# Modulation by blocks of 128 features, three weight tiles multiplied while they load, and other numbers in the planner

## The chip, the cores and the metric

One core of a Trainium2 chip runs the whole kernel. The metric is device time in microseconds (us), the median of three timed runs of one launch. The engines are TensorE (PE: matmuls; PEld: its weight loads), VectorE (DVE), ScalarE (ACT), GpSimd (POOL) and SyncE (SP), which here issues every transfer, on one queue.

## The reference, cut to what matters

One inference step of a hybrid decoder layer: 512 prompt tokens and 8 x 4 sample tokens, 544 columns in all, model width 1024.

```python
def layer_front(x, c, w_cond, b_cond, w_in):
    shift, scale, gate = jnp.split(jax.nn.silu(c) @ w_cond + b_cond, 3, axis=-1)
    h = x * (1 + scale[:, None]) + shift[:, None]
    return gate, split_columns(h @ w_in)
```

`c` has 9 rows: one for the prompt, one for each sample sequence. `w_cond` is 1024 x 3072, `w_in` is 1024 x 11280. The columns of `h @ w_in` feed two branches: windowed softmax attention (24 heads in 3 groups) and a gated delta rule (8 heads: a causal convolution of width 4, silu, a chunked triangular solve, a state that passes through 4 chunks of 128 tokens; its decays and betas, the gates, come from 16 further columns of `w_in`). Then

```python
merged = jax.nn.sigmoid(ga) * (ya @ w_branch_a) + jax.nn.sigmoid(gb) * (yb @ w_branch_b)
r = ALPHA * x + gate * (merged @ w_out)         # then a LayerNorm over the features
```

The kernel also returns the shifted key/value caches, the convolution tails and the delta states.

## The kernel before, in words

**How the work is laid out.** Features lie on the partitions, 8 blocks of 128 (`KT`); tokens are the columns. `h` is kept as a pair: `hhi`, rounded to fp32r, and `hlo`, the rest. Every weight tile (128 output columns of `w_in`, 128 x 1024 in SBUF) is split in the same way into `hi` and `lo` by `split`: a copy on ACT and a subtraction on DVE. A tile's product over one half of the tokens (272 columns) is 8 blocks x 3 matmuls (`hi` with `hhi`, `hi` with `hlo`, `lo` with `hhi`) into one PSUM buffer, so a tile has 48 matmuls. `stream` in `body` goes through the tiles (jobs) in a fixed order: three of delta head 0, nine of attention, and so on. A job's `evac` takes each half out of PSUM. PSUM has 8 buffers: 2 `pp` for the stream, 2 `pd`, 3 `pg`, 1 `pb`.

**The front.** Before any tile, scale and shift must be known. `cond_product` multiplies silu(c) (tile `cs`, 32 columns with 9 in use) with `w_cond`, which comes in 8 transfers of 1 MiB (tile `wc`): first the 4 with the scale columns, then the 4 with the shift columns. `to_features` turns each result (`Y`) into columns over the partitions by small products with a selecting constant (`cst`, result in `pd`). Only then is `h` formed block by block: on DVE `xT` times scale plus shift, on ACT the copy `hhi`, on DVE the difference `hlo`.

**The gates.** `gates` multiplies `h` with the 16 gate columns (32 matmuls of 272 columns into `pg`), brings the result to tokens on partitions (`cg`, `abT`) and computes softplus, exponentials and running sums in some 25 small DVE and ACT instructions on 34 columns; their tiles lie in two pools (`gtab`, `gt`), and the attention's pool `ap` opens only once both are closed.

**What sets the order.** The program is first recorded: `Threads` interleaves the generators (delta rule, delta blocks, gates, attention, stream, sample work) on a clock that counts matmul cost, and each instruction gets a rank. Then `Recorder.schedule` plans it: a list scheduler with costs and latencies for each engine (`cost`, `WAKE`, `margin`), a transfer queue, tile buffers and a model of TensorE's clock; at each step the engine that is free first takes its ready instruction of the lowest rank. What comes out is a fixed order on each engine. All instructions are issued by `emit`, so the profile gives one line, L638, for nearly all of them; they are told apart by their tiles.

**The end of the first phase.** The tiles of the delta rule and of the attention lie in pools (`dl`, `ap`) that are closed after the eighth head's rule. The buffers `zt` of the later gate tiles (`zp`) are opened after that. The delta rule ends, for each head, with a root (`rn`) and a scaling (`orow`) that is written out.

Of the kernel before, what the change touches and what calls it, by code (L numbers as in the profile page):

```python
# [38 lines left out]
EARLY_A, EARLY_B = 7, 2  # L39
S0B = 7  # L40
# [203 lines left out]
class Recorder:  # L244
# [4 lines left out]
    OVER = {"ve": 0.08, "se": 0.10, "ge": 0.05}  # L249
    HOLD = 1.0  # L250
# [3 lines left out]
    def __init__(self):  # L254
        self.ops, self.events, self.rank, self.now, self.idle = [], [], 0, 0.0, 0.0
        self.group = None
        self.scratch = {}
# [8 lines left out]
    def add(self, engine, name, args, kw):  # L266
        op = Op(len(self.ops), engine, name, args, kw, self.rank)
        op.group, op.part, op.epoch = self.group, self.rank, len(self.events)
# [65 lines left out]
    def cost(self, op, args):  # L334
# [5 lines left out]
        op.two = len(tensors) > 1 and not in_psum  # L340
        op.transfer = None
# [18 lines left out]
        elif e == "ve":  # L360
            if op.name == "reciprocal":
                c = 0.15 + 6.25e-3 * n
            elif op.name == "memset":
                c = 0.06 + 0.83e-3 * n
            elif len(tensors) == 1 and not in_psum and op.name in ("tensor_scalar", "tensor_copy"):
                c = 0.15 + 0.76e-3 * n
            else:
                c = 0.152 + 1.05e-3 * n
            op.cost, op.late = c - 0.08, 0.08
        elif e == "se":  # L370
            c = (0.185 if in_psum else 0.21) + 0.83e-3 * n
            a = 0.15 if "accum_out" in op.kw else 0.0
# [42 lines left out]
    def schedule(self):  # L415
# [9 lines left out]
        for op in ops:  # L425
            op.left = len(op.deps)
            for d in op.deps:
# [22 lines left out]
        def candidate(op):  # L450
# [22 lines left out]
            for d, data in op.deps.items():  # L473
# [3 lines left out]
                else:  # L477
                    r = max(r, p.end + (0.06 if data and op.engine != "pe" else 0.0))
            for t in op.tiles:
                if t.ops[0] == op.n:  # L480
# [29 lines left out]
        while done < len(ops):  # L510
# [31 lines left out]
            else:  # L542
                op = None
                if e == "pe" and rounded[0] and not avail[e][0][-1].rounded:

                    if t - min(x[-1].ready for x in avail[e] if not x[-1].rounded) < self.HOLD:
# [5 lines left out]
                if op is None:  # L552
                    op = pop(avail[e])[-1]
            if op.group is not None:
# [7 lines left out]
            if e == "pe":  # L562
# [8 lines left out]
                busy.append((t, t + c))  # L571
            if op.two and e in port:
# [8 lines left out]
            op.done = t + c + op.late  # L581
            free[e] = op.end
# [108 lines left out]
def body(ctx, tc, io):  # L691
# [80 lines left out]
    def cond_rows(part, k0, nk):  # L772
        return io["w_cond"][k0 * 128:(k0 + nk) * 128, part * D:(part + 1) * D].rearrange("(k p) c -> p k c", p=128)

    def to_features(pv, k, rows):

        for i in range(4):
            pe.matmul(pv[:, k + i, 0:9], rows[:, 128 * i:128 * i + 128], C("selc"), start=True, stop=True)

    f16 = lambda t: t[:, :128].rearrange("p (a b) -> p a b", b=16)  # L780
# [10 lines left out]
    gctx = ExitStack()  # L791
    d1 = pool(gctx, "gtab", 1)
    tables["g"] = d1.tile([128, CONST[1].shape[1]], F32, name="cg")
    dta = d1.tile([128, 2, 34], F32, name="dta")
    with ExitStack() as fctx:
        fr = pool(fctx, "front", 1)
        cT = fr.tile([128, KT, 32], F32, name="cT")
        ve.memset(cT, 0.0)
        sp.dma_start(cT[:, :, 0:9], io["cT"])
# [5 lines left out]
        ve.tensor_mul(cs, cT, th)  # L805
        xT = fr.tile([128, KT, NT], F32, name="xT")
        pieces = {}
        for part in (1, 0):
            for k in range(0, KT, 2):
                pieces[part, k] = fr.tile([128, 2, D], F32, name="wc", bufs=8)  # L810
                sp.dma_start(pieces[part, k], cond_rows(part, k, 2))
                if (part, k) == (1, 6):
                    sp.dma_start(cst, io["const"])
        sp.dma_start(wab, io["w_ab"])
        raws[0] = wraw.tile([128, D], F32, name="wt", tag="wraw")
        sp.dma_start(raws[0], io["w_in"][TILE_AT["b", 0, 1]])
        weights[0] = split(raws[0], D, ve)
        for k in range(0, KT, 2):
            sp.dma_start(xT[:, k:k + 2], io["xT"][:, k:k + 2])
# [4 lines left out]
        def load_front(part):  # L824
            for k in range(0, KT, 2):
                for n in range(2):
                    for q in range(2):
                        yield k + q, n, pieces[part, k][:, q, 512 * n:512 * n + 512]

        sc = fr.tile([128, KT, 9], F32, name="sc")  # L830
        sh = fr.tile([128, KT, 9], F32, name="sh")
        for part, t in ((1, sc), (0, sh)):
            ps = [pp(), pp()]
            take(cond_product(part, load_front, ps), 99)
            pv = f16(pd())
            bias = bT[:, 8 * part:8 * part + 8, None].to_broadcast([128, 8, 9])
            for n in range(2):
                Y = fr.tile([128, 512], F32, name="Y", bufs=2)
                if n:
                    se.activation(Y, ps[n], AF.Copy)  # L840
                else:
                    ve.tensor_copy(Y, ps[n])
                to_features(pv, 4 * n, Y)
            if part:
                ve.scalar_tensor_tensor(t, pv[:, :, 0:9], 1.0, bias, op0=OP.add, op1=OP.add)
            else:
                ve.tensor_add(t, pv[:, :, 0:9], bias)
        sp.dma_start(bnw, io["b_norm_w"])
        ve.tensor_scalar(hbnw, bnw, 0.5, None, op0=OP.mult)
        xs = xT[:, :, SEQ:].rearrange("p k (b t) -> p k b t", t=4)  # L850
        per_token = lambda t, k, n: t[:, k:k + n, 1:9, None].to_broadcast([128, n, 8, 4])
        for k in range(0, KT, 2):
            ve.tensor_mul(xs[:, k:k + 2], xs[:, k:k + 2], per_token(sc, k, 2))
# [1406 lines left out]
```

## Time and profile before

| | us |
|---|---|
| median of 3 runs | 984.84 (983.84 to 985.1) |
| the profiled execution's own time | 984.89 |
| its span, first to last instruction | 982.8 |
| busy in the span: PE, PEld | 922.8 (94%), 842.9 (86%) |
| busy: DVE, ACT, POOL | 739.4 (75%), 413.6 (42%), 75.7 (8%) |
| mean granted TensorE clock | 0.980 of full speed |

Times in the rows are from the span's start. Matmul records overlap: a busy matmul shows longer than the distance to the next one, and it is the distance that adds up. An fp32 matmul leaves two records, an fp32r matmul one. "Idle before" is the time for which the engine had nothing to do ahead of a row, with what ended it.

### The profile page before, as it was taken

The numbers are of one execution on the slowest core, as the hardware profiler recorded it, in microseconds if no ns is written. First come the engines' busy times: TensorE is split into PE (matmuls) and PEld (weight loads), VectorE is DVE, ScalarE is ACT, GpSimd is POOL, SyncE is SP. The second block draws the span as 40 slices with busy tenths as digits, with TensorE's granted clock in tenths as the row PEclk, the third lists the DMA queues.
The fourth block names the chain that finished last, engine by engine and source line by source line (L and its number), as shares of the span: only waits on it lengthen the run. The fifth ranks groups of instructions, "written<-read, shape, count | busy, mean of one in ns | idle before, by whom it ended". The sixth has DMA issues, their size and how long they took to land. (4 is left out here: it accounts for less than half of the span.)

```text
span 982.8 us, 20665 instructions
## 1 busy us (share of the span) xinstructions
PE 922.8 (94%) x8070; PEld 842.9 (86%) x8070; DVE 739.4 (75%) x1620; ACT 413.6 (42%) x971; POOL 75.7 (8%) x176
## 2 busy tenths in 40 slices
PE   4899999999999999999999799998999999999896
PEld 1699988999978988888988698798899999997785
DVE  0575565866889999699987866655799899847658
ACT  0364447543546443456443545433342222234420
POOL 0120001101001410000200100001010000000000
PEclk8799999999999999999999999998999999999998
DMA  9676755675877887968777665359689899975513
GB/s 359 206 249 207 218 188 201 215 196 186 290 250 230 264 247 247 311 219 281 267 247 241 206 196 182 134 188 324 249 286 340 322 418 406 352 242 175 189 38 109
DMA packets 106340, 237.76 MB, mean 242 GB/s; under 512 B 30898, under 2 KB 62140, under 8 KB 103556
## 3 DMA queue, kind: packets, MB, share of 16 engines
q1 hardware_dynamic: 106244, 236.45, 71.2%
q8 instruction: 63, 1.03, 0.4%
q14 instruction: 33, 0.27, 0.1%
HBM read 220.40 MB, written 103.70 MB: 330 GB/s over the span
## 5 line engine op out<-in xcount | busy, mean ns | idle before, releaser
L638 PE MATMUL pp<-hhi,hi 128*128 128x272 f32 x1408 | 414.9, 295 | 8.3 <-DVE spare L638 2.6
L638 PE MATMUL pp<-hhi,lo 128*128 128x272 f32 x1408 | 414.1, 294 | 0.0
L638 PE MATMUL pp<-hlo,hi 128*128 128x272 f32 x1408 | 412.1, 293 | 0.6 <-DVE hlo L638 0.6
L638 PEld LDWEIGHTS pp<-hhi,hi 128*128 128x128 f32 x1408 | 268.1, 191 | 12.5 <-DVE spare L638 2.9
L638 PEld LDWEIGHTS pp<-hlo,hi 128*128 128x128 f32 x1408 | 268.0, 190 | 2.5 <-DVE hlo L638 0.9
L638 PEld LDWEIGHTS pp<-hhi,lo 128*128 128x128 f32 x1408 | 267.7, 190 | 2.0 <-issue 1.0
L638 ACT ACTIVATE hi<-wt 128x1024 fp32r<-128x1024 f32 (+1 forms) x104 | 106.7, 1026 | 169.6 <-PE pp L638 148.1
L638 DVE TENSOR_TENSOR lo<-wt,hi 128x1024 fp32r<-128x1024 f32 (+1 forms) x104 | 122.4, 1177 | 63.1 <-ACT hi L638 60.7
L638 DVE SCALAR_TENSOR_TENSOR acc<-ext,cw,acc 128x568 f32<-128x568 f32 x72 | 57.5, 799 | 2.5 <-ACT acc L638 0.9
L638 ACT ACT_TABLE_LOAD x34 | 43.6, 1283 | 12.5 <-DMA cT<-in_cT 7.9
L638 ACT ACTIVATE P<-P,st 128x256 f32<-128x256 f32 (+1 forms) x64 | 31.3, 489 | 34.9 <-DVE st L638 34.8
L638 DVE TENSOR_TENSOR slab<-slab 128x512 f32<-128x512 f32 (+1 forms) x66 | 42.4, 667 | 4.6 <-DMA slab<-in_vs 2.0
L638 DVE TENSOR_REDUCE slab<-slab 128x8 f32<-128x512 f32 (+2 forms) x66 | 42.5, 656 | 0.6 <-ACT slab L638 0.4
L638 ACT ACTIVATE zt<-pp 128x272 f32<-128x272 f32 x48 | 18.6, 388 | 50.8 <-PE pp L638 38.7
L638 POOL COPY cx<-ext 128x3 f32<-128x3 f32 (+1 forms) x48 | 32.4, 704 | 90.8 <-ACT ext L638 90.6
L638 PE MATMUL pp<-ybl,hi 128*128 128x272 f32 x128 | 37.0, 289 | 0.0
L638 PE MATMUL pg<-k,q 64*128 64x128 f32 (+1 forms) x192 | 34.4, 331 | 2.8 <-DVE st L638 2.7
L638 PE MATMUL pp<-ybh,lo 128*128 128x272 f32 x128 | 37.0, 289 | 0.0
L638 PE MATMUL pp<-ybh,hi 128*128 128x272 f32 x128 | 36.8, 287 | 0.0
L638 PEld LDWEIGHTS pg<-k,q 64*128 64x128 f32 x192 | 23.2, 186 | 10.5 <-DVE st L638 4.5
L638 DVE CUSTOM_DVE_ANT_0 P<-pg,bias 128x256 f32<-128x256 f32 (+1 forms) x64 | 24.0, 403 | 8.5 <-PE pg L638 8.4
L638 ACT ACTIVATE ext<-pp 128x272 f32<-128x272 f32 (+2 forms) x72 | 20.0, 315 | 23.2 <-PE pp L638 19.3
(395 smaller groups left out, 1585.0 us busy)
## 6 DMA issues: line engine op xcount, KB each, us to landing
out_kv_s<-in_cache SPq DMA_DIRECT2D x144, 512.0 KB
wt<-in_w_in SPq DMA_DIRECT2D x88, 512.0 KB
out_kv_s<-in_cache SPq DMA_DIRECT2D x24, 496.0 KB
wc<-in_w_cond SPq DMA_DIRECT2D x8, 1024.0 KB
slab<-in_ks SPq DMA_DIRECT2D x32, 256.0 KB
slab<-in_vs SPq DMA_DIRECT2D x32, 256.0 KB
kv<-in_ks SPq DMA_DIRECT2D x16, 512.0 KB
kv<-in_vs SPq DMA_DIRECT2D x16, 512.0 KB
```

What stands on the lines that cost most here:

```text
L638: getattr(real[x.engine], x.name)(*map(arg, x.args), **{k: arg(v) for k, v in x.kw.items()})
```

## The change

Five edits.

1. **The front by feature blocks.** The host lays out the scale and shift columns of `w_cond` as `w_mod`: 8 blocks of 1 MiB, block k holding all 1024 rows of the 128 shift and 128 scale columns of features 128k to 128k+127. Each block is loaded into its own tile `wm`, multiplied (8 matmuls of 256 columns instead of a share of 512-column ones), brought over the partitions by 2 small products and applied to block k of `xT` at once, so `hhi[k]` and `hlo[k]` exist before block k+1 is needed. The input `cT` is padded to 32 columns by the host, and the memset of `cT` goes.
2. **Three tiles between.** The weight tiles of the first three jobs load between the blocks (`FIRST`), are split there, and after each block their 18 matmuls over that block are issued (rank 9). The six halves take both `pp`, all three `pg` and the `pb` buffer. `stream` then only evacuates these jobs. Loads of the next jobs are held back to 28 us on the planner's clock (`BEHIND`).
3. **The gates in borrowed tiles.** The gates' tiles come from the pool `opool` (nine buffers, tag `o`) which the first tiles' weights also borrow; `gtab` and `gt` are gone, and `ap` opens without waiting for the gates. The block of zeros is half as wide and is written in two transfers.
4. **The planner's numbers.** VectorE: 1.045 in place of 1.05 ns per element, and 0.055 us more for an instruction with a per-partition operand and two tensors or for a transpose; ScalarE: 0.155 in place of 0.185 us from PSUM, 0.07 in place of 0.15 for an accumulated output, 0.08 for a per-partition operand; a new wait `AGAIN` between dependent instructions of one engine (0.11 VectorE, 0.14 ScalarE, where it was 0.06).
5. **The planner's rules.** An instruction on a PSUM buffer waits until the other engines' last instruction on that buffer is done (`turn`); a GpSimd copy counts VectorE's hold on the shared port; `hold` becomes a property of an instruction and is 0 for the last block's products.

```diff
+FIRST = (1, 2, 3)
+BEHIND = 28.0
...
+    AGAIN = {"pe": 0.0, "ve": 0.11, "se": 0.14, "ge": 0.11, "sp": 0.0}
...
-                c = 0.152 + 1.05e-3 * n
+                c = 0.152 + 1.045e-3 * n
+            if op.name == "scalar_tensor_tensor" and pointer or op.name == "transpose":
+                c += 0.055
...
-            c = (0.185 if in_psum else 0.21) + 0.83e-3 * n
-            a = 0.15 if "accum_out" in op.kw else 0.0
+            c = (0.155 if in_psum else 0.21) + 0.83e-3 * n
+            a = (0.07 if "accum_out" in op.kw else 0.0) + (0.08 if pointer else 0.0)
...
-                    r = max(r, p.end + (0.06 if data and op.engine != "pe" else 0.0))
+                    r = max(r, p.end + (self.AGAIN[op.engine] if data else 0.0))
...
+                turn = max((d + self.WAKE[e] for b in op.banks for x, d in b.turn.items() if x != e), default=0.0)
+                if turn > t + 0.001:
+                    op.ready = turn
+                    push(wait[e], (turn, op.n))
+                    continue
...
+        wm = [fr.tile([128, KT, 256], F32, name="wm", bufs=6) for _ in range(KT)]
+        for k in range(KT):
+            sp.dma_start(wm[k], io["w_mod"][k])
+            if k == 0:
+                sp.dma_start(cst, io["const"])
+            if k % 2 == 0:
+                sp.dma_start(xT[:, k:k + 2], io["xT"][:, k:k + 2])
+            if k in FIRST:
+                i = FIRST.index(k)
+                raws[i] = wraw.tile([128, D], F32, name="wt", tag="wraw")
+                sp.dma_start(raws[i], io["w_in"][TILE_AT["b", 0, (1, 0, 2)[i]]])
...
+        ahead = {0: [pp(), pp()], 1: [pg(), pg()], 2: [pg(), pb_()]}
...
+        for k in range(KT):
+            pc = pd()
+            rec.hold = 0.0 if k == KT - 1 else rec.HOLD
+            with rec.together():
+                for i in range(KT):
+                    q = i % 4
+                    pe.matmul(pc[32 * q:32 * q + 32, 0:256], cs[:, i, :], wm[k][:, i, :], start=(i < 4), stop=(i >= 4),
+                              tile_position=(0, 32 * q))
+            Y = fr.tile([128, 256], F32, name="Y", bufs=2)
+            se.activation(Y, pc[:, 0:256], AF.Copy)
+            pv = pc[:, 256:288].rearrange("p (a b) -> p a b", b=16)
+            for u in range(2):
+                pe.matmul(pv[:, u, 0:9], Y[:, 128 * u:128 * u + 128], C("selc"), start=True, stop=True)
+            m = mod[:, k]
+            ve.tensor_add(m, pv[:, :, 0:9], mb[:, k, :, None].to_broadcast([128, 2, 9]))
+            per_token = lambda u: m[:, u, 1:9, None].to_broadcast([128, 8, 4])
+            ve.tensor_mul(xs[:, k], xs[:, k], per_token(1))
+            ve.tensor_add(xs[:, k], xs[:, k], per_token(0))
+            h = xT[:, k]
+            ve.tensor_scalar(h[:, :SEQ], h[:, :SEQ], m[:, 1, 0:1], m[:, 0, 0:1], op0=OP.mult, op1=OP.add)
+            se.activation(hhi[:, k, :], h, AF.Copy)
+            ve.tensor_sub(hlo[:, k, :], h, hhi[:, k, :].bitcast(F32))
+            rec.rank = 9
+            for i in range(3):
+                a, b = weights[i][k]
+                for w, x in ((a, hhi), (b, hhi), (a, hlo)):
+                    for n in range(2):
+                        pe.matmul(ahead[i][n][:, :HF], w, x[:, k, n * HF:(n + 1) * HF],
+                                  start=(k == 0 and w is a and x is hhi), stop=(k == KT - 1 and x is hlo))
+            rec.rank = 0
...
+            if i in ahead:
+                weights.pop(i)
+                for n, ps in enumerate(ahead.pop(i)):
+                    job.evac(n, ps[:, :HF])
+                    yield 0
+                done[0] += 1
+                threads.set(job.over, 0.0)
+                continue
...
-        d1 = pool(gctx, "gt", 1)
+        free = lambda name, dt=F32: op.tile([128, NT], dt, name=name, tag="o")
...
-    threads.run(lambda: ab["over"])
-    gctx.close()
```

**The order on TensorE at the start.** What stands first on PE before (`wc` pieces of `w_cond`, `cst`,`Y` the turn over the partitions, then the first tile's products into `pp`):

```order
1 L638 MATMUL pp<-wc,cs 32x512 x16
2 L638 MATMUL pd<-cst,Y 128x9 x8
3 L638 MATMUL pp<-wc,cs 32x512 x16
4 L638 MATMUL pd<-cst,Y 128x9 x8
5 L638 MATMUL pp<-hhi,hi 128x272 x2
6 L638 MATMUL pp<-hlo,hi 128x272
```

All 32 products with `w_cond` and both turns stand ahead of the first tile's first product. The same place now (`wm` is a block of `w_mod`; `whi`, `wlo` are borrowed weights of a first tile):

```order
1 L658 MATMUL pd<-wm,cs 32x256 x8
2 L658 MATMUL pd<-cst,Y 128x9 x2
3 L658 MATMUL pd<-wm,cs 32x256 x8
4 L658 MATMUL pp<-hhi,whi 128x272 x2
5 L658 MATMUL pd<-cst,Y 128x9 x2
6 L658 MATMUL pp<-hhi,wlo 128x272 x2
7 L658 MATMUL pp<-hlo,whi 128x272 x2
8 L658 MATMUL pd<-wm,cs 32x256 x8
9 L658 MATMUL pp<-hhi,whi 128x272 x2
```

The first tile's products of block 0 now stand between the second and the third block of the modulation. Counted along the order, 103 of the first three tiles' 144 products stand ahead of the last block's turn, and the 32 products of the gates follow when 143 are done.

**The order on ScalarE at the last block.** Before, the eight copies `hhi` stand together, behind the first weight tile's copy (`ea` is the gates' exponential):

```order
4 L638 ACTIVATE hi<-wab 128x8x16
5 L638 ACTIVATE hi<-wt 128x1024
6 L638 ACTIVATE Y<-pp 128x512
7 L638 ACTIVATE hhi<-xT 128x544 x8
8 L638 ACTIVATE ea<-dta 128x34
```

Now, at the last two blocks (`cg` is the borrowed tile with the gates' inputs; `hi<-wt` is the fourth tile's copy):

```order
20 L658 ACTIVATE hhi<-xT 128x544
21 L658 ACTIVATE Y<-pd 128x256
22 L658 ACTIVATE cg<-cg 128x34
23 L658 ACTIVATE hi<-wt 128x1024
24 L658 ACTIVATE hhi<-xT 128x544
25 L658 ACTIVATE ext<-pp 128x272
```

The gates' exponential and the fourth tile's copy stand between the last block's `Y` and its `hhi`, and each reads a tile that is loaded after the last block.

**The order on TensorE at the end of the eighth head's rule.** Before (`vn`, `kr`, `QKd`, `S`, `KQ` are the last chunk of the delta rule):

```order
3670 L638 MATMUL pp<-hlo,hi 128x272
3671 L638 MATMUL pd<-vn,kr 128x128
3672 L638 MATMUL pd<-vn,QKd 128x128
3673 L638 MATMUL pd<-S,KQ 128x128
3674 L638 MATMUL pp<-hhi,lo 128x272
3675 L638 MATMUL pp<-hhi,hi 128x272
```

Counted along the order, the rule ends here after 3140 products of the stream; the 67th tile, the first whose `zt` comes from `zp`, ends at 3216. Now (`kq` belongs to the sample part of the delta rule):

```order
3742 L658 MATMUL pp<-hhi,lo 128x272
3743 L658 MATMUL pd<-vn,kr 128x128
3744 L658 MATMUL pd<-vn,QKd 128x128
3745 L658 MATMUL pd<-S,KQ 128x128
3746 L658 MATMUL pb<-kq 128x256 x2
3747 L658 MATMUL pp<-hhi,hi 128x272
```

It ends after 3216 products, with both `pp` buffers full of the 67th tile.

## Rows read from the trace of the kernel before

**Rows 1.** Busy time by stage, whole core: sum, PE, PEld, DVE, ACT, POOL, clock, DMA, GB/s.

```profile
0.00:45.00 45.00, 27.21 (x146) 16.16 (x147) 15.46 (x38) 9.09 (x15) 3.15 (x13) 0.81 0.80 301
45.00:100.00 55.00, 55.00 (x440) 53.51 (x439) 31.70 (x81) 29.37 (x71) 5.16 (x14) 1.00 0.73 222
...
300.00:560.00 260.00, 244.16 (x2269) 225.48 (x2268) 233.49 (x564) 126.30 (x314) 32.21 (x66) 1.00 0.77 253
```

**Rows 2.** Waits of PE, first 45 us: total us, times, longest.

```profile
PE pp L638 <- DMA wc<-in_w_cond: 13.4, 4, 10.6
```

**Rows 3.** Timeline of the front: start, us, engine, operation, count, idle before.

```profile
0.73 0.40 SPq L638 DMA_DIRECT2D xT<-in_xT  x1
...
20.89 3.58 PE L638 MATMUL pd<-cst,Y 128*128 128x9 f32 x16 [0.78 <-DVE Y L638]
...
24.40 5.59 PE L638 MATMUL pp<-wc,cs 128*32 128x512 f32 x32
...
28.92 0.16 PEld L638 LDWEIGHTS pp<-wc,cs 128*32 128x32 f32 x8 [0.91 <-DMA wc<-in_w_cond]
...
31.31 0.58 ACT L638 ACTIVATE Y<-pp 128x512 f32<-128x512 f32 x1
...
35.15 0.82 PE L638 MATMUL pp<-hhi,hi 128*128 128x272 f32 x2 [2.15 <-ACT hhi L638]
```

**Rows 4.** Busy time in stretches of 2 us, columns as in Rows 1.

```profile
18.00:20.00 2.00, 1.83 (x8) 0.20 (x8) 0.00 (x0) 0.00 (x0) 0.00 (x0) 0.51 1.04 414
...
28.00:30.00 2.00, 1.99 (x20) 0.17 (x10) 0.29 (x1) 0.31 (x1) 0.82 (x5) 0.93 1.04 402
...
40.00:42.00 2.00, 2.00 (x11) 2.00 (x11) 2.00 (x4) 0.58 (x2) 0.00 (x0) 0.52 0.00 0
42.00:44.00 2.00, 2.00 (x18) 2.00 (x18) 1.28 (x3) 0.66 (x1) 0.00 (x0) 1.00 0.00 0
```

**Rows 5.** Timeline of PE at 40.6 and at 62.4 us.

```profile
40.59 0.43 PE L638 MATMUL pp<-hhi,hi 128*128 128x272 f32 x1
40.82 0.43 PE L638 MATMUL pp<-hlo,hi 128*128 128x272 f32 x1
...
62.41 0.29 PE L638 MATMUL pp<-hhi,lo 128*128 128x272 f32 x1
62.54 0.50 PE L638 MATMUL pg<-g,cg 128*128 128x32 f32 x4
```

**Rows 6.** Tile xT, first 45 us: count, ns min/median/max, starts, forms.

```profile
L638 DVE TENSOR_SCALAR xT<-xT,sc,sh x8: 539/540/541, 33.9 to 42.1; 128x512 f32<-128x512 f32 x8
L638 ACT ACTIVATE hhi<-xT x8: 638/642/659, 34.4 to 42.6; 128x544 fp32r<-128x544 f32 x8
L638 DVE TENSOR_TENSOR hlo<-xT,hhi x8: 714/718/726, 35.8 to 43.3; 128x544 fp32r<-128x544 f32 x8
...
L638 DVE TENSOR_TENSOR xT<-xT,sc x4: 215/222/226, 24.8 to 34.8; 128x64 f32<-128x64 f32 x4
```

**Rows 7.** Tile wt, first 80 us, columns as in Rows 6.

```profile
L638 ACT ACTIVATE hi<-wt x7: 1042/1057/1061, 30.3 to 78.1; 128x1024 fp32r<-128x1024 f32 x7
L638 DVE TENSOR_TENSOR lo<-wt,hi x7: 1222/1226/1227, 31.4 to 79.2; 128x1024 fp32r<-128x1024 f32 x7
```

**Rows 8.** Costliest DVE groups, 300 to 560 us: busy, mean ns, idle before.

```profile
L638 DVE SCALAR_TENSOR_TENSOR acc<-ext,cw,acc 128x568 f32<-128x568 f32 x37 | 29.4, 794 | 0.2
```

**Rows 9.** Timeline at the end of the eighth head's rule, by engine.

```profile
660.76 0.39 PE L638 MATMUL pd<-S,KQ 128*128 128x128 f32 x2
...
666.21 0.68 DVE L638 TENSOR_TENSOR orow<-pd,rn 128x512 f32<-128x512 f32 x1
...
667.29 0.59 PE L638 MATMUL pp<-hhi,hi 128*128 128x272 f32 x1 [2.63 <-DVE spare L638]
```

**Rows 10.** Busy time, 665 to 670 us, columns as in Rows 1.

```profile
665.00:670.00 5.00, 2.71 (x12) 2.71 (x13) 4.41 (x8) 1.16 (x2) 1.22 (x3) 0.66 0.60 179
```

More of the change, by code (lines that the diff above doesn't have):

```diff
@@ L340, in cost @@
         op.two = len(tensors) > 1 and not in_psum
+        pointer = any(size(v) == 1 for v in op.ins)
         op.transfer = None
@@ L426, in schedule @@
             op.left = len(op.deps)
+            op.banks = [t for t in op.tiles if t.pool.side == "psum"]
+            for t in op.banks:
+                t.turn = {}
             for d in op.deps:
@@ L544, in schedule @@
                 if e == "pe" and rounded[0] and not avail[e][0][-1].rounded:
-                    if t - min(x[-1].ready for x in avail[e] if not x[-1].rounded) < self.HOLD:
+                    if all(t - x[-1].ready < x[-1].hold for x in avail[e] if not x[-1].rounded):
                         x = min((x for x in avail[e] if x[-1].rounded), default=None)
@@ L581, in schedule @@
             op.done = t + c + op.late
+            for b in op.banks:
+                b.turn[e] = op.done
             free[e] = op.end
@@ L770, in cond_product, with cond_rows @@
             yield
[L772 to L780, printed above, removed]
+    def cond_rows(k0, nk):
+        return io["w_cond"][k0 * 128:(k0 + nk) * 128].rearrange("(k p) c -> p k c", p=128)
     def split(raw, n, eng):
@@ L790, in body @@
     wab = consts.tile([128, KT, 16], F32, name="wab")
[L791 to L794, printed above, removed]
+    cg = op.tile([128, NT], F32, name="cg", tag="o")
+    tables["g"], dta = cg[:, :CONST[1].shape[1]], cg[:, NT - 68:].rearrange("p (u c) -> p u c", u=2)
+    ahead = {}
     with ExitStack() as fctx:
@@ L805, in body @@
         ve.tensor_mul(cs, cT, th)
+        mb = fr.tile([128, KT, 2], F32, name="mb")
+        ve.tensor_copy(mb[:, :, 0], bT[:, 0:8])
+        ve.tensor_scalar(mb[:, :, 1], bT[:, 8:16], 1.0, None, op0=OP.add)
         xT = fr.tile([128, KT, NT], F32, name="xT")
[L807 to L813, printed above, removed]
-        sp.dma_start(wab, io["w_ab"])
[L815 to L819, printed above, removed]
+        wm = [fr.tile([128, KT, 256], F32, name="wm", bufs=6) for _ in range(KT)]
[9 more added lines that the diff above has]
+                sp.dma_start(raws[i], io["w_in"][TILE_AT["b", 0, (1, 0, 2)[i]]])
+        sp.dma_start(wab, io["w_ab"])
         sp.dma_start(tables["g"], io["const_g"])
@@ L822, in body @@
         sp.dma_start(dta, io["dta"])
[L824 to L847, printed above, removed]
+        for i in range(3):
+            if i == 2:
+                hi, lo = split(raws[i], D, ve)
+                weights[i] = [(hi[:, 128 * k:128 * k + 128], lo[:, 128 * k:128 * k + 128]) for k in range(KT)]
+                continue
+            weights[i] = []
+            for u in range(2):
+                hi = op.tile([128, NT], F32R, name="whi", tag="o")[:, :512]
+                lo = op.tile([128, NT], F32R, name="wlo", tag="o")[:, :512]
+                raw = raws[i][:, 512 * u:512 * u + 512]
+                se.activation(hi, raw, AF.Copy)
+                ve.tensor_sub(lo, raw, hi.bitcast(F32))
+                weights[i] += [(hi[:, 128 * k:128 * k + 128], lo[:, 128 * k:128 * k + 128]) for k in range(4)]
@@ L848, in body @@
+        rec.hold = rec.HOLD
         sp.dma_start(bnw, io["b_norm_w"])
         ve.tensor_scalar(hbnw, bnw, 0.5, None, op0=OP.mult)
[L850 to L853, printed above, removed]
-        for k in range(0, KT, 2):
-            ve.tensor_add(xs[:, k:k + 2], xs[:, k:k + 2], per_token(sh, k, 2))
@@ L856, in body @@
-        for k in range(KT):
-            h = xT[:, k]
-            ve.tensor_scalar(h[:, :SEQ], h[:, :SEQ], sc[:, k, 0:1], sh[:, k, 0:1], op0=OP.mult, op1=OP.add)
-            se.activation(hhi[:, k, :], h, AF.Copy)
-            ve.tensor_sub(hlo[:, k, :], h, hhi[:, k, :].bitcast(F32))
     class Job:
@@ L1965, in body @@
     blocks = threads.add(chain(delta_blocks, 8), 1)
-    ab = threads.add(gates(), 2)
+    threads.add(gates(), 2)
     threads.add(stream(60 + 4 + EARLY_B), 9)
-    threads.run(lambda: ab["over"])
-    gctx.close()
     ap = pool(actx, "ap", 1)
```

57 lines of the change are left out of this document (30 added, 27 removed).

## The prediction

> **What bounds the kernel now.** I read the busy time by stage first. From 45 to 100 us TensorE is busy for all 55.00 us, from 300 to 560 for 244.16 of 260, but in the first 45 us only for 27.21, at a mean clock of 0.81 [rows 1]. So TensorE bounds the kernel once it has work, and what is saved ahead of its first product moves everything behind it. Next the waits: four waits for pieces of `w_cond` take 13.4 us [rows 2]. The timeline says why: the last piece lands at 28.92, and the first product of a weight tile starts at 35.15, behind the turn over the partitions and the modulation [rows 3]. The queue is the limit till then: 414 and 402 GB/s [rows 4]. Last the clock: the front runs at 0.51 at 18 us, is back near full speed at 28 to 30 after TensorE had been busy without a gap since 20.89, falls again in the waits ahead of 35.15, and products run 0.23 us apart until about 42, 0.125 apart (0.13 in the row) from there [rows 3 to 5].
>
> The mark against which I measure is 62.54, where TensorE starts the gates' sums: by then it has done the 144 products of the first three tiles and the gates' 32 [rows 5]. It does the same work in both kernels; the question is when.
>
> **Part 1, the blocks and the tiles between.** *Transfers.* Ahead of the last piece of `w_cond` stood 10.21 MB (from the shapes: `w_cond` 8.39, one pair of `xT` 0.56, two weight tiles 1.05, the rest 0.22); it landed 28.2 us after the first issue at 0.73 [rows 3]. Ahead of the last block now stand 12.50 MB: all of `xT` (2.23) and three weight tiles (1.57). The 2.29 MB more at 0.41 MB per us [rows 4] are 5.6 us: the last block lands at 34.5.
>
> *The chain behind the last block.* Eight products of 256 columns: the 16 of 512 columns in the second half took 5.59 us at mostly half clock [rows 3], 0.35 each, so 0.35 x 8 / 2 = 1.4, or 0.7 at full clock. `Y`, half as wide as the 0.58 us one: 0.35. Two turns: 16 records in 3.58 us, so 4 are 0.9, or 0.45 at full clock [rows 3]. On VectorE an addition, the two sample steps at 0.22 each and the 512-column step at 0.54: 1.2. `hhi` 0.64, `hlo` 0.72 [rows 6]. With five hand-overs between engines at 0.1 (an estimate) this is 4.6 to 5.7. Then the order: ScalarE does the fourth tile's copy (1.06) ahead of `hhi`, and VectorE its subtraction (1.23) [rows 7] ahead of `hlo`. The tile lands behind the block, some 2 us later (0.84 MB). That adds up to 1.2. `hlo` of the last block: 39.1 to 41.4, I take 40.3.
>
> *TensorE till then.* Borrowed weights of the first tile are there at about 13.6: 3.49 MB at 0.41 after the same start are 12.5, and a half tile's copy and subtraction add 1.1 (half of 1.06 and 1.23). From there to 40.3 it has 126 products (15.8 us at 0.125) and some 6.5 blocks of modulation at 1.15 (7.5), 23.3 us at full clock in a stretch of 26.7. But it starts at half clock; the trace gave full speed back after about 6.7 us without a gap (35.15 to some 41.9 [rows 3, 4]), which costs 3.4. That just fits. Behind `hlo` come 14 of the last block's 18 products, 1.8, and the gates' 32, 4.0: 46.1. The 16 records that bring the gates over the partitions, at no more than 0.125, are 2.0: the mark is reached at 48.1 and not 62.54: **14.4 us**. If chain and clock both go well it is 46 (16.5), if the clock comes back 6 us later, 51 (11.5).
>
> *Does the lead last?* Behind the mark TensorE is full till 100 us [rows 1], if others feed it. Three tiles are evacuated at once and the gates' small instructions fall into the same stretch. VectorE was busy for 31.70 us of 55 [rows 1]; packed into 55 - 14.4 = 40.6 us it still fits, so the cover is thin but there. A wait of TensorE for the gates' sums is possible: 0 to 3 us, I take 1. The three held `pp`, `pg` and `pb` buffers cost nothing as long as ScalarE evacuates them under the gates' 4.0 us (six halves at about 0.4, as wide as a half of `Y`: 2.4).
>
> **Part 2, the gates' tiles.** The same instructions on other addresses; the zeros cost one more issue on SP, behind which only a cache move waits. `ap` opens earlier, which only adds freedom. Bound 0.3 either way, I take 0.
>
> **Part 3, the planner.** Work is the same from the mark on, only the order differs. Two places. At the end of the first phase the eighth head's rule now ends after 3216 products of the stream instead of 3140. Before, those 76 products (9.5 us) lay behind it as cover for its root, its scaling (`orow` from 666.21, 5.4 us after the last product at 660.76) and the opening of the pools. Still TensorE stood for 2.63 us at 667.29, for a gate tile of VectorE, and then ran at 0.66 [rows 9, 10]. Now both `pp` buffers are full when the rule ends: nothing covers the 5.4 us and the first evacuation behind them. With 0.4 + 0.4 for that I get 6.2, less the 2.63 that go if VectorE is not crowded: **+3.5** (0, if the pools open sooner, to 7, if the output must land first).
>
> From 300 to 560 VectorE is busy for 233.5 of 260 us [rows 1], and TensorE's 15.8 us of gaps are its waits. The old numbers charge a 568-column step with a per-partition operand 0.748 us; it takes 0.794 [rows 8]. 37 of them are 1.7 us that the old plan did not see in its most crowded stretch. The new numbers see it. I take **-2** (-5 to +3, since any new order has its own waits).
>
> The sum against the execution profiled: 984.9 - 14.4 + 1 + 3.5 - 2 = **973.0**; its own time is the median of the runs within 0.1.
>
> **The rivals.**
>
> *A. The front stays at half clock.* For it: at 10 to 18 us, with a piece of work for each transfer and a wait behind it, the clock fell to 0.51 [rows 4]; now every block is such a piece. Against it: there is a backlog of products from 13.6 on, so the waits should vanish. Its time: at half clock until 6.7 us behind the last block (41.2), TensorE does 13.8 of its 23.3 us of work from 13.6 on; the other 9.5 end at 50.7, and 1.8 + 4.0 + 2.0 later, at 58.5, stands the mark: a lead of 4.0, and 984.9 - 4.0 + 2.5 = 983.4. Half of that loss gives 978.
> The Trainium skill's page "TensorE: Matmul & The Clock Gate", section "HAM oscillation — how this bites in real kernels", describes this: a loop whose products per tile are shorter than the transfer wait starts every tile at the low clock. The trace agrees as far as the stretch from 10 to 20 us goes; it does not show what a backlog of products does to it.
>
> *B. The end of the phase does not stall and the new plan saves its 5.* For it: the old stall there was VectorE's merging, which the new order ends earlier. 984.9 - 15.5 - 5 = 964.
>
> *C. Slower: sample attention.* Its last product stood after 2634 products of the stream; now it stands at 2849, and its nine borrowed buffers are wanted from the 63rd tile on, at 2976. The cover shrinks from 342 to 127 products, 16 us. If VectorE falls behind its plan by more than that, each us is lost: 28 us (16 of cover, 12 of the lead left) bring it back to 985, from there it is slower, and 35 give 992. Against it: with 26.5 idle us from 300 to 560 [rows 1] VectorE would have to be far off plan.
>
> *D. The change doesn't do what it says:* the planner could have put every product behind the blocks. The order shows that it did not, so this has no chance beside A.
>
> **How the numbers follow.** Forecast (968 to 977): 0.62. A in part (977 to 982): 0.12; A in full (983.4): 0.05. B: 0.14. C: 0.07. Most bounds of the forecast (mark 46 to 51, phase end 0 to 7, plan -5 to +3) lie within 963 to 981; beyond it remain A in full, C and a little of B, about 0.15. The range is 963 to 981. A measurement of this kernel can tell about 0.2% (2 us) from no change: faster 0.88 (forecast, B, A in part), same 0.05, slower 0.07.
>
> **What would show it.** Right: the last block lands near 34.5; products of the first tiles start near 14; the clock is full from about 21 on; the gates' sums start near 48; TensorE is full from there to 100; a wait of some 6 us where the eighth rule ends. Wrong: a clock near 0.5 up to 35 us; gaps of TensorE ahead of each block; a wait for `hhi` behind ScalarE's copy longer than 2 us; long waits for the gates' sums near 60; waits for `slab` between 500 and 600.

## The result, and the profile after

The changed kernel takes 974.32 us (median of 4 runs, 972.59 to 977.22) against 984.97 for the kernel before on the same chip: a ratio of 0.9888, 95% interval 0.9852 to 0.9925. The forecast was 973.0. The execution profiled took 975.1 us, 9.8 less than that of before.

The front first. Busy time by stage of the changed kernel, columns as in [rows 1]:

```profile
0.00:45.00 45.00, 36.48 (x305) 28.68 (x306) 19.52 (x56) 15.14 (x30) 1.98 (x13) 1.00 0.83 323
45.00:100.00 55.00, 54.59 (x433) 52.00 (x432) 34.84 (x93) 29.05 (x72) 3.46 (x14) 1.00 0.73 220
...
300.00:560.00 260.00, 247.68 (x2252) 228.60 (x2251) 236.62 (x566) 130.31 (x325) 38.07 (x70) 0.98 0.78 257
```

TensorE is busy for 36.48 us of the first 45, where it was 27.21 [rows 1]. Its waits there, against [rows 2]:

```profile
PE pd L658 <- DMA wm<-in_w_mod: 8.0, 2, 7.3
```

Two waits for blocks, the second over at 11.48; for the last six blocks it does not wait. TensorE's timeline shows why, against [rows 3, 5]:

```profile
13.41 0.82 PE L658 MATMUL pp<-hhi,whi 128*128 128x272 f32 x2
...
18.74 0.66 PE L658 MATMUL pp<-hhi,wlo 128*128 128x272 f32 x2
...
20.66 0.41 PE L658 MATMUL pg<-hhi,wlo 128*128 128x272 f32 x2
...
36.51 0.51 PE L658 MATMUL pd<-cst,Y 128*128 128x9 f32 x4
36.95 1.07 PE L658 MATMUL pd<-wm,cs 128*32 128x256 f32 x16
37.95 0.39 PE L658 MATMUL pp<-hhi,wlo 128*128 128x272 f32 x1
...
42.63 0.42 PE L658 MATMUL pp<-hhi,whi 128*128 128x272 f32 x2
...
48.62 0.28 PE L658 MATMUL pg<-hlo,hl 128*32 128x272 f32 x1
48.83 0.61 PE L658 MATMUL pg<-cg,abT 32*128 32x16 f32 x4
```

The first product starts at 13.41 instead of 35.15, products come at full spacing from 20.66 on, the last block's 18 products start at 42.63 with no gap before them, and the 176th product (144 and the gates' 32) ends at 48.75.

Then a stop that I had not foreseen, in the third head's rule. The changed kernel's timeline from 264 to 277 us, SP, POOL, DVE and PE:

```profile
264.59 1.39 SPq L658 DMA_DIRECT2D slab<-in_ks  x3
266.08 0.38 SPq L658 DMA_DIRECT2D dO<-orow  x1
...
272.26 0.53 POOL L658 MEMSET XF<- 128x512 f32 x1 [4.19 <-DMA dO<-orow]
...
272.82 0.30 DVE L658 STREAM_TRANSPOSE XF<-Tc 32x128 f32<-32x128 f32 x1 [4.15 <-POOL XF L658]
...
276.11 0.18 PE L658 MATMUL pd<-W,XF 32*32 32x32 f32 x1 [2.52 <-DVE W L658]
```

And in stretches of 2 us, the seventh number being the clock:

```profile
274.00:276.00 2.00, 0.00 (x0) 0.00 (x0) 1.86 (x6) 0.89 (x2) 0.00 (x0) 1.00 1.19 469
276.00:278.00 2.00, 1.77 (x27) 1.17 (x28) 1.94 (x5) 0.33 (x2) 0.03 (x1) 0.58 0.31 121
...
288.00:290.00 2.00, 2.00 (x9) 1.11 (x8) 0.58 (x1) 0.46 (x2) 0.00 (x0) 0.51 0.41 87
290.00:292.00 2.00, 2.00 (x13) 1.38 (x13) 0.97 (x3) 0.00 (x0) 0.00 (x0) 1.00 0.99 339
```

The eight heads' output rows (`orow`) lie in the buffer of `XF`, a tile of the delta rule that POOL clears for each head. The second head's rows are issued to memory at 266.08, behind three loads of `slab`, and have landed at 272.2; until then POOL can't clear `XF` for the third head, VectorE stands behind POOL, TensorE behind VectorE. It stands 2.52 us and then works at half clock until 290. By windows of 2 us from 272 to 292 (time not busy, plus the busy time times the clock's shortfall) this place costs 9.4 us, 2.6 of standing and 6.7 of half clock. In the kernel before the same write (issued at 271.32, POOL's clearing at 273.62) took 2.3 us, and TensorE was busy for 9.16 of the 10 us from 270 on.

The Trainium skill's page "DMA: Bandwidth & Descriptors", section "Queues, rings and completion order", says that each DMA engine takes the descriptors of a ring in their order. By that a write waits behind the loads issued ahead of it; the 6.1 us here behind three loads of 256 KB, against 2.3 us in the kernel before behind six writes of 32 KB, agree with it. No run moves this write alone, so that the loads ahead of it make the difference, and not those behind it, is not shown.

The end of the first phase, TensorE, VectorE and TensorE again, against [rows 9]:

```profile
662.94 0.39 PE L658 MATMUL pd<-S,KQ 128*128 128x128 f32 x2
663.16 1.03 PE L658 MATMUL pb<-kq 128*128 128x256 f32 x4
...
665.64 0.69 DVE L658 TENSOR_TENSOR orow<-pd,rn 128x512 f32<-128x512 f32 x1
...
667.64 0.39 PE L658 MATMUL pp<-hhi,hi 128*128 128x272 f32 x1 [3.45 <-DVE zt L658]
```

A stop of 3.45 us where 6.2 were forecast.

The new order has one more expensive place, in the sixth head's rule: TensorE stands four times for 1.11 to 1.85 us between 544.66 and 557.29, and runs at half clock from 549.4 to 563.0:

```profile
550.00:555.00 5.00, 2.74 (x10) 1.85 (x9) 4.66 (x15) 1.47 (x7) 0.00 (x0) 0.50 0.16 45
```

### Where the lead goes

I number the 4832 records of 128x272 on TensorE's timeline in their order and compare, at equal number, the time of before with that of the other kernel. Up to the 1300th and from the 3300th on, nearly equal work lies ahead of a number, so the differences there are leads; between them the heads' rules stand at other places in each order, and single values are off by several us. The leads are read to about 0.2 us, each from the one execution that was profiled, while the ratios are of medians. What that is worth the row of e9 shows, a kernel with the very order of before and one address changed: 3.4 us at the 4400th product and 5 us of loss lie between two executions of one order. "Loss" is the time not busy plus the half-clock loss between 100 and 700 us, by windows of 2 us. The names of the experiments are explained below.

| kernel | front | planner | 300th | 900th | 1300th | 1500th | 3300th | 4400th | loss | ratio |
|---|---|---|---|---|---|---|---|---|---|---|
| before | old | old | 0 | 0 | 0 | 0 | 0 | 0 | 34 | 1 |
| e9 | old | before's order | 0.5 | 0.3 | 0.2 | -1.3 | -3.1 | -3.4 | 39 | 1.002 |
| after | new | new | 11.1 | 8.6 | 9.3 | 0.5 | 8.2 | 7.9 | 34 | 0.9888 |
| e1 | new | old | 10.1 | 7.4 | 6.0 | 5.0 | 19.9 | 18.4 | 29 | 0.9793 |
| e13 | new | old, 1 ns | 8.7 | 3.0 | 1.3 | 4.1 | 4.0 | 1.5 | 38 | 0.9928 |
| e2 | old | new | -1.2 | -0.8 | -0.2 | 4.3 | 18.0 | 20.3 | 24 | 0.9713 |
| e12 | old | new, 1 ns | -0.8 | -0.5 | 0.2 | 4.3 | 13.5 | 12.8 | 24 | 0.9848 |
| e7 | new | new, 1 ns | 11.3 | 8.9 | 10.8 | 9.7 | 22.8 | 22.5 | 23 | 0.9781 |
| e8 | old | old, 1 ns | -0.4 | -0.4 | -1.4 | -0.8 | 0.3 | 0.9 | 41 | 0.9957 |
| e4 | new, products behind | new | -5.0 | -6.3 | -6.6 | -4.3 | 4.3 | 4.9 | 31 | 0.9870 |
| e3 | new | new, orow moved | 11.9 | 9.5 | 10.4 | 11.0 | 25.6 | 23.2 | 19 | 0.9719 |
| e5 | new | after's order | 11.6 | 9.2 | 10.5 | 11.4 | 15.3 | 12.1 | 32 | 0.9854 |
| e10 | new | after's order | 11.7 | 9.3 | 11.0 | 11.9 | 21.4 | 20.6 | 24 | 0.9820 |
| e11 | new | e3's order | 11.3 | 8.9 | 9.7 | 9.5 | 28.6 | 27.6 | 13 | 0.9712 |

### The profile page after: what moved, and what is told of

Its sections match the earlier page's. It is cut to its first block, busy times and chain, and to the rows that moved or that the text cites. A ratio compares the mean times of both kernels' runs of the same rounds, so it can differ in the third digit from the quotient of the medians.

```text
span 973.2 us, 20825 instructions
## 1 busy us (share of the span) xinstructions
PE 929.4 (96%) x8134; PEld 849.9 (87%) x8134; DVE 740.4 (76%) x1635; ACT 416.6 (43%) x981; POOL 76.3 (8%) x176
## 3 DMA queue, kind: packets, MB, share of 16 engines
q8 instruction: 64, 1.05, 0.4%
## 4 chain that ended last, share of the span: by engine, by line
PE 65%; DVE 20%; DMA 8%; ACT 3%; issue 3%; SPq 2%; POOL 0%; DVEq 0%; ACTq 0%; POOLq 0%
PE pp L658 46%; PE pg L658 10%; PE pd L658 6%; DVE slab L658 3%; DVE lo L658 3%; PE pb L658 3%; DVE r L658 2%; SPq L658 2%; DMA slab<-in_ks 2%; DVE Tb L658 1%; DVE tmp L658 1%; DMA out_kv_s<-in_cache 1%; DVE NTs L658 1%; DVE acc L658 1%; DMA wm<-in_w_mod 1%
## 5 line engine op out<-in xcount | busy, mean ns | idle before, releaser
L658 PE MATMUL pp<-hhi,hi 128*128 128x272 f32 x1360 | 400.5, 294 | 7.8 <-DVE zt L658 4.2
L658 PE MATMUL pp<-hhi,lo 128*128 128x272 f32 x1360 | 399.6, 294 | 0.0
L658 PE MATMUL pp<-hlo,hi 128*128 128x272 f32 x1360 | 398.8, 293 | 0.0
L658 PEld LDWEIGHTS pp<-hhi,hi 128*128 128x128 f32 x1360 | 258.5, 190 | 13.7 <-DVE zt L658 4.6
L658 PEld LDWEIGHTS pp<-hlo,hi 128*128 128x128 f32 x1360 | 258.5, 190 | 3.3 <-issue 2.3
L658 PEld LDWEIGHTS pp<-hhi,lo 128*128 128x128 f32 x1360 | 258.2, 190 | 1.2 <-issue 0.6
L658 ACT ACTIVATE hi<-wt 128x1024 fp32r<-128x1024 f32 (+1 forms) x102 | 104.5, 1024 | 160.8 <-PE pp L658 135.0
L658 DVE TENSOR_TENSOR lo<-wt,hi 128x1024 fp32r<-128x1024 f32 (+1 forms) x102 | 120.1, 1177 | 42.6 <-ACT hi L658 41.2
L658 POOL COPY cx<-ext 128x3 f32<-128x3 f32 (+1 forms) x48 | 36.5, 789 | 96.9 <-ACT ext L658 96.7
L658 PE MATMUL pg<-k,q 64*128 64x128 f32 (+1 forms) x192 | 37.6, 335 | 0.5 <-DVE st L658 0.2
L658 ACT ACTIVATE ext<-acc 128x568 f32<-128x568 f32 x24 | 16.2, 674 | 27.9 <-DVE acc L658 25.5
```

The lines of the kernel that those rows point to most:

```text
L658: getattr(real[x.engine], x.name)(*map(arg, x.args), **{k: arg(v) for k, v in x.kw.items()})
```

## The experiments

Theory: the products between the blocks make a lead of some 14 us, and the order that the planner then writes takes or gives a few. Rivals: the new numbers earn or cost the larger part; or the shorter chain behind the last transfer makes the lead, wherever the products stand. All ratios are to the kernel before on the same chip.

### e1: old numbers on the new front; e2: new numbers on the old front

```diff
-                    r = max(r, p.end + (self.AGAIN[op.engine] if data else 0.0))
+                    r = max(r, p.end + (0.06 if data and op.engine != "pe" else 0.0))
...
-                c = 0.152 + 1.045e-3 * n
-            if op.name == "scalar_tensor_tensor" and pointer or op.name == "transpose":
-                c += 0.055
+                c = 0.152 + 1.05e-3 * n
...
-            c = (0.155 if in_psum else 0.21) + 0.83e-3 * n
-            a = (0.07 if "accum_out" in op.kw else 0.0) + (0.08 if pointer else 0.0)
+            c = (0.185 if in_psum else 0.21) + 0.83e-3 * n
+            a = 0.15 if "accum_out" in op.kw else 0.0
```

This is e1's edit of the changed kernel; the turn on a PSUM bank and the port rule go with it. e2 makes the reverse edit in the kernel before.

> The changed kernel with the planner's old costs and rules: only parts 1 and 2 of the change are left. My theory (front 14.4 of lead, 1 lost at the gates' sums, planner +1.5 net): 984.9 - 14.4 + 1 = 971.5, so 1 to 2 us under the changed kernel's 974.3. Rival 1, the new plan itself costs the lead (its two half-clock stretches at 277 and 549 us come from it, 6 us or more): 966 to 969. Rival 2, the new numbers earn some 4 of the 10 us: 977 to 980.

> The kernel before with the planner's new costs and rules and its old front: part 3 of the change alone. My theory (+3.5 at the end of the phase, -2 where VectorE is crowded): 986.5. Rival 1, the new plan costs 5 or more: 990 or above. Rival 2, the new numbers earn about 4: 980 to 981.

e1: 965.27 (964.08 to 969.03), ratio 0.9793, interval 0.9756 to 0.9831. e2: 957.75 (955.44 to 961.97), ratio 0.9713, 0.9677 to 0.9748. My theory misses both, by 6 and by 29 us. The table says where: on the new front the lead at the 300th product is there with either set of numbers (11.1 and 10.1), on the old front it isn't (-1.2); what differs comes between the 1300th and the 3300th. And the two parts don't add: the new numbers cost 9 us on one front and earn 28 on the other. A term with a fixed sign for the planner can't be right.

### e3: the output rows in another buffer

```diff
-        orow = dl.tile([128, 4, 128], F32, name="orow", tag="XF", bufs=1)
+        orow = vr
```

> The changed kernel, but the eight heads' output rows (orow) are written over the head's vr, which is no longer needed, instead of into XF's buffer, so that POOL's clearing of XF need not wait for the write of orow to memory. If the stop of 2.52 us at 276 and the 12.5 us at half clock behind it (6 us of work) come from that wait, the lead that falls from 13 to about 4.5 us between 260 and 310 stays, 8 us at 310; half of it may be given back in the crowded stretch: 967 to 972. Rival, VectorE bounds the stretch from 300 to 560 whatever comes before: 974 to 975.

958.64 (957.48 to 959.95), ratio 0.9719, 0.9687 to 0.975. Some 16 us under the changed kernel, where 2 to 7 were expected: the stop at 274 is gone (lead 11.0 at the 1500th product, not 0.5), but the planner knows of the freed buffer and wrote another order from the second head's rule on, which has no stop at 545 to 560 either. So it is no measure of the wait alone; e5 is.

### e4: the products of the first three tiles behind the last block

```diff
-            rec.rank = 9
-            for i in range(3):
+        rec.rank = 9
+        for i in range(3):
+            for k in reversed(range(KT)):
...
-                                  start=(k == 0 and w is a and x is hhi), stop=(k == KT - 1 and x is hlo))
-            rec.rank = 0
+                                  start=(k == KT - 1 and w is a and x is hhi), stop=(k == 0 and x is hlo))
+        rec.rank = 0
```

> The changed kernel, with the 144 products of the first three tiles forced behind the last block (each sum begins with the eighth block of features), everything else of the front as it is. If the products between the blocks are what makes the lead: last hlo near 40, then 176 products (22 us) and some 3 us at half clock, so the 176th ends near 64 to 65 instead of 48.75, and the time is 988 to 992. Rival, the shorter chain behind the last transfer makes the lead and the products could stand anywhere: 974 to 979.

974.31 (968.98 to 977.81), ratio 0.987, 0.9829 to 0.991: by its time the rival would have won. The timeline of its front says otherwise (the last row is the third head's rule):

```profile
41.24 0.82 PE L658 MATMUL pp<-hhi,whi 128*128 128x272 f32 x2 [1.81 <-ACT hhi L658]
41.86 0.43 PE L658 MATMUL pp<-hhi,wlo 128*128 128x272 f32 x1
...
60.52 0.29 PE L658 MATMUL pg<-hlo,hl 128*32 128x272 f32 x1
...
273.92 0.18 PE L658 MATMUL pd<-W,XF 32*32 32x32 f32 x1 [2.17 <-DVE XF L658]
```

The last `hlo` ends at 42.27, as in the changed kernel (42.58), so transfers and chain are the same; but the first product starts at 41.24 and the 176th ends at 60.7, 11.9 us behind the changed kernel's 48.75, and at the 300th it is 5.0 behind the kernel before, 16 behind the changed one. The products between the blocks make the lead. The order that this kernel then got gained 11.2 on before from the 900th to the 4400th product, where the changed kernel's lost 0.7. It has the same wait for `orow` as the changed kernel (issued at 266.68, POOL clears `XF` at 272.60, TensorE stands 2.17 us), but only 3.4 us of half clock behind it. Of the 11.2 only 2.5 are standing and half clock. The other 8.7 lie in the busy time itself: between these two products TensorE has 5914 records here and 5918 in the kernel before, and its busy time less the half-clock loss is 619 us against 628 (e9, with before's order, 626; the changed kernel 626; e2 616). So an order also sets how close the small products lie to each other, which the column of losses does not show; what brings them closer, no run takes apart.

### e7, e8, e12, e13: a cost of the planner moved by 1 ns

```diff
-                c = 0.152 + 1.045e-3 * n
+                c = 0.153 + 1.045e-3 * n
```

(in e8 and e13 with 1.05e-3.) Nothing that the chip does depends on it but the order.

> The changed kernel with one planner cost moved by 1 ns (a VectorE step's fixed part 0.153 for 0.152), which means nothing for the chip but gives another order from the 1045th row of TensorE on. If the new numbers and rules as such cost the 9 us by which the old numbers beat them on this front (965.3 against 974.3), this stays at 972 to 977. If the stalls of an order are a matter of chance, it lies anywhere from 955 to 980, and a difference of more than 3 us from 974.3 shows it.

> The kernel before with the same cost moved by the same 1 ns. If the new numbers earn the 27 us that they gave on the old front (957.8 against 985.0) by seeing the steps rightly, this stays at 983 to 988. If it is the chance of an order, it lies anywhere from 955 to 990, and a difference of more than 3 us from 985.0 shows it.

> Old front, new numbers and rules, with the planner's cost of a VectorE step moved by 1 ns. If the 27 us of the first such order (957.8) are the numbers' own, this is 955 to 963. If they are mostly the chance of one order, it lies between 963 and 985.

> New front, old numbers and rules, with the same cost moved by 1 ns. With 965.3 for the first such order and 985.0 and 978.7 for the old front with old numbers: if the front's lead of 14 us lasts whatever the order, this is 962 to 972. If the chance of one order is as large as the lead, it can be 975 or more.

e7: 961.36 (960.36 to 962.13), ratio 0.9781, 0.9749 to 0.9813. e8: 978.72 (976.9 to 983.89), 0.9957, 0.9933 to 0.9981. e12: 969.21 (968.27 to 973.34), 0.9848, 0.9817 to 0.9879. e13: 978.08 (972.65 to 983.82), 0.9928, 0.99 to 0.9955.

By the ratios, taken to 985 us, the nanosecond moved the new front with the new numbers by 10.5 us, the old with the old by 4.2, and the two mixed kernels by 13.3 each: in three of the four cases about as much as the whole gain of the change (11 us), or more. With two orders for each combination, the new numbers stand at a mean ratio of 0.9808 against 0.9920 for the old ones (11 us), the new front at 0.9848 against 0.9880 (3 us). With four orders on a side that differ by 4 to 13 us in their pairs, neither is settled by these times. That the new front gives 9 to 12 us up to the 300th product is settled, by the timelines. In e13 it melts to 1.3 by the 1300th. e7 also has the wait for `orow` (issued at 267.29, POOL clears `XF` at 274.90); TensorE stands 1.53 us for it, and no half clock follows right behind it.

### e5, e9: the changed kernel's order kept, one wait taken away

```diff
         orow = dl.tile([128, 4, 128], F32, name="orow", tag="XF", bufs=1)
+        orow.base.instead = vr.base
 ...
+            if t.real is None and hasattr(t, "instead"):
+                t.real = t.instead.real
```

The planner still sees `XF`'s buffer, and every engine's order stays; only the address differs. e9 is the same edit in the kernel before.

> The changed kernel with every engine's order kept, row for row; only the address of the eight heads' output rows (orow) is another: the head's own vr instead of XF's buffer. What goes is one kind of wait, POOL's clearing of XF behind the write of orow to memory. If that wait makes the stop at 274 to 290 us (9.0 us by windows of 2 us: 2.5 of standing, 6.5 of half clock), the lead at the 1500th product goes from 0.5 to 8 or 9 us and holds: 965 to 967. Rival, the VectorE-crowded stretch from 310 to 350 takes it back: 972 to 975.

> The kernel before, every engine's order kept, with orow at vr's address as in the same experiment on the changed kernel. POOL waits there 36 us in 6 waits for the write of orow, but no stop of TensorE begins behind one: 984 to 986. If these waits cost it something all the same: 975 to 982.

e9: 986.33 (981.31 to 991.25), ratio 1.002, 0.9994 to 1.0045: as expected, in the kernel before the wait cost nothing. e5: 968.97 (967.5 to 970.86), 0.9854, 0.9816 to 0.9893, only 3.3 us under the changed kernel by the ratios, whose intervals overlap. But the stop has gone entirely; the lead at the 1500th product is 11.4 instead of 0.5, and still 22.7 against 10.1 at the 3200th. In e5, POOL and the same stretch as above:

```profile
265.98 0.53 POOL L660 MEMSET XF<- 128x512 f32 x1
```

```profile
274.00:276.00 2.00, 2.00 (x20) 1.43 (x17) 1.94 (x5) 0.81 (x3) 0.13 (x1) 1.00 0.90 308
276.00:278.00 2.00, 2.00 (x18) 1.88 (x16) 1.78 (x7) 0.92 (x3) 0.06 (x1) 1.00 0.49 150
```

So the crowded stretch behind it does not take the gain back, and the rival falls: 10.9 us at that place, against the 9.4 of the windows. What stood in the wait itself is 2.5 of them; the rest is half clock, and that is not the same behind each such wait: e4 and e7 stand 2.17 and 1.53 us for it and pay 1.7 and 0 us of half clock. What e5 loses again, it loses at the end of the phase (timeline of e5, ACT and PE):

```profile
658.36 1.28 ACT L660 ACT_TABLE_LOAD   x1 [5.54 <-DMA dO<-vr]
659.65 0.69 ACT L660 ACTIVATE zt<-pp 128x272 f32<-128x272 f32 x2
...
660.57 0.59 PE L660 MATMUL pp<-hhi,hi 128*128 128x272 f32 x1 [8.97 <-DVE zt L660]
```

The next phase's `zt` takes the address where the eighth head's rows now lie, and ScalarE has to wait until they are in memory: the end that the prediction had named as its bound of 7, made by the edit itself.

### e10, e11: the eighth head's rows left where they were

```diff
-        orow.base.instead = vr.base
+        if h < 7:
+            orow.base.instead = vr.base
```

In e11 the same in e3: `orow = vr if h < 7 else dl.tile(... tag="XF" ...)`.

> As the same-order kernel without the wait, but only heads 0 to 6 put their rows over vr; the eighth head's stay in XF's buffer as in the changed kernel. There the lead of 10.9 us at the 1500th product was still 12 at the 3200th and fell to 4 at the 3300th, and ScalarE stood 5.54 us for the write of the eighth head's rows, whose address the next phase's zt takes. If that address is the cause, the stop at the end of the phase shrinks from 8.97 us to about 3.5 and the time is 961 to 964. Rival, the end of the phase waits for something that is late whatever the lead: 968 to 970.

> As the kernel that was planned with orow over vr (958.6), with the eighth head's rows left in XF's buffer; TensorE's order is the same row for row. It lost 9.9 us at 644 to 658. If 5.5 of them are the write of the eighth head's rows, as in the same-order kernel: 951 to 955, the fastest of all. Rival, that loss is the rule's own chain: 957 to 959.

e10, the end of the phase (ACT, PE), and under it the same place of e11:

```profile
652.52 1.28 ACT L660 ACT_TABLE_LOAD   x1
653.82 0.69 ACT L660 ACTIVATE zt<-pp 128x272 f32<-128x272 f32 x2
...
654.75 0.59 PE L660 MATMUL pp<-hhi,hi 128*128 128x272 f32 x1 [3.46 <-DVE zt L660]
```

```profile
649.12 0.40 PE L658 MATMUL pp<-hhi,hi 128*128 128x272 f32 x1 [3.92 <-DVE zt L658]
```

The stop shrinks from 8.97 to 3.46 us in e10, as expected, and from 6.92 in e3 to 3.92 in e11. The medians move less: e10 966.89 (962.32 to 969.98), ratio 0.982, 0.9786 to 0.9854, where 961 to 964 was expected (the execution profiled is its fastest, at 962.3); e11 956.44 (954.7 to 959.09), 0.9712, 0.9682 to 0.9742, where 951 to 955 was. The mechanism is shown; its worth in the medians, about 2 us each, lies within the intervals. e10 stands 6.7 us under the changed kernel by the ratios, whose intervals just touch: with the order kept, that is the best estimate of what the two waits cost. e11 is the fastest kernel of all, 17 us under the changed one; e2, which has none of the new front, is level with it.

## Why the prediction was right, and where it was not

**The front (14.4, less 1 for the gates' sums): the mechanism holds, the size was 2 too large.** The 176th product was to end at 46.1 and ended at 48.75. Neither transfer nor chain did that: the last `hlo` ended at 42.58, not 40.3, and still TensorE never waited for it. It was TensorE's own work that I had priced too low: a block's 16 and 4 records take 1.00 + 0.44 = 1.44 us at full spacing (36.51 to 37.95), where I took 1.15; over six and a half blocks that is 1.9 of the 2.65. The wait at the gates' sums was 0.28, and all standing from 45 to 100 us 0.41, instead of 1. So the lead past the gates is 11.1 at the 300th product, where 14.4 - 1 = 13.4 was forecast.

**The clock** came back between 19 and 20.7, as drawn (about 21): the products of 18.74 stand 0.225 apart, those of 20.66 0.13. Rival A is out: behind 11.48 TensorE had no wait, the third block still ran at half clock (16 records in 1.94 us at 16.26), and from the fourth on each ran at full (1.07 at 22.00). What I had said of the kernel before from 10 to 20 us was too neat: of the four pieces there three ran at half clock for all or most of their time (1.93, 1.81 and 1.94 us), the one at 15.62 at full (1.06), and the waits between them, 0.55 to 1.49 us, were not longer than the products. The Trainium skill's "TensorE: Matmul & The Clock Gate", section "HAM oscillation — how this bites in real kernels", describes loops without such a backlog; this front has one and shows no falling back.

**The last block** was to land at 34.5 and its chain to take up to 1.2 more for the fourth tile. VectorE did put that tile's subtraction (40.72 to 41.94) ahead of the last `hlo`; it cost TensorE nothing. When the block landed the trace does not show, since TensorE came to it only at 36.95. In e4, whose blocks are issued within 0.4 us of the same times, TensorE starts the last one at 34.47 behind a step of VectorE: it had landed by then.

**The end of the phase (+3.5): the step failed.** The stop was 3.45 us, not 6.2. From the rule's last product (662.94) to `orow` it was 2.7 us, where I had carried over the 5.4 of the kernel before; there VectorE's merging lay in between (2.25 us from the root's end on ScalarE to `rn` on VectorE), which rival B had named. And there was cover after all: the sample part's products (`pb<-kq`) ran until 664.2. With the half clock behind it the place loses 5.6 us in both kernels: the term is 0.

**The crowded stretch (-2): the step failed too.** What the order does is of another size. Where the stop and its echo at the end of the phase are taken out of it (e10, in its fastest execution; the medians put it some 4 us lower), it gains 10.4 us on before from the 1300th to the 3300th product (11.0 to 21.4), although the costly place near 550 stays in it; the stop takes 10.9 away. Neither stood in my sum, since I weighed the two places that I knew and not the waits that a new order makes. The stop was to be found: `orow` shares `XF`'s buffer, and in the trace of before POOL stands 36.2 us for its writes. I had passed over that because it cost TensorE nothing there.

**So 973.0 is right by one term that holds (13.4, measured 11) and by the rest coming out near the forecast's +1.5 by chance** (measured: 11.1 at the 300th product, 9.8 at the end; the 1.3 between them is less than two executions of one order differ by). The range of 963 to 981 held, but 1 ns in a cost would have given 961.4, outside it; that is near rival B's 964, by another way. And the 2 us that I held for measurable were too few: the interval of the ratio is 3.6 us wide to each side. Rival C did not happen: among the changed kernel's waits of TensorE of 0.2 us or more from 45 us on, none is for `slab`. Rival D was out by the order.

## What to carry to other kernels

Where a planner writes the order, run the kernel with a cost moved by nothing before you believe a gain of a per cent: here a nanosecond was worth 4 to 13 us. Judge a change in one stage by the lead at a fixed point of the work behind that stage, not by the time at the end. And look for buffers that a write to memory shares with the next step: such a wait is free until the write stands behind other transfers, and then it stops three engines in a row; keeping the order and changing the address alone prices it.

## What the runs showed of the hardware

- After the stop of 2.52 us at 273.6 TensorE was busy without a gap by its records and still ran at 0.50 until 290, for over 12 us; after the stops of 3.45 us that ends at 667.64 and of 2.63 us that ends at 667.29 (before) it was back in some 6 us at most. In e4, behind 2.17 us at the same place, the half clock lasted 3.4 us.
- A long stop is not needed for it. In e9 the half clock lasts from 634.5 to 644.7, and in the 6 us before it TensorE stands for no more than 0.34 us at a time; it works on products of 32x32 there. The kernel before, with the same order, shows full clock at that place. What the length of these stretches hangs on, no run shows. A row of e9 in that stretch:

```profile
636.00:638.00 2.00, 2.00 (x10) 1.75 (x10) 0.30 (x2) 1.14 (x5) 0.00 (x0) 0.50 0.00 0
```

- In the front of the changed kernel until 20 us, and of e4 until 47.2, the clock column reads 1.00 while products stand 0.22 us or more apart, which elsewhere goes with 0.52 [rows 4, 5]. There the spacing of equal records is the better clock.
- A write of 256 KB landed 2.3 us after its issue in one kernel and 6.1 in the other, with six writes of 32 KB ahead of it in the one and three loads of 256 KB in the other.
